# Two groups of matmul operands of an encoder kernel get new places in SBUF: the gated outputs 64 bytes lower and the memory's tiles 32 bytes higher, modulo 256

## Chip, cores and metric

The kernel runs on one core of a Trainium2 chip, in one launch. The metric is the device time of the whole program in microseconds. A version is timed in several runs on the same chip, and the median counts.

## What is computed

The reference is an encoder trunk of two layers over 256 positions of width 2048. In each layer a pre-normalized input `h` is projected by one large matrix into mixer columns, cross-attention queries and a gate. The mixer is a multi-scale mean with a grouped matrix in layer 0, and a gated DeltaNet in both directions over chunks of 64 in layer 1. Beside it stands a cross-attention of 4 heads into 256 memory tokens.

```python
for i in range(DEPTH):
    h = rmsnorm(x, norm_w[i])
    kv = rmsnorm(mem, mem_norm_w[i]) @ w_kv_mem[i]
    ...
    if i % 2 == 0:
        y = pooling_branch(h, pool_w_in[j], pool_w_group[j], pool_scale[j], mem_k, mem_v)
    else:
        y = deltanet_branch(h, dn_w_in[j], dn_conv_w[j], dn_a_log[j], dn_dt_bias[j], dn_norm_w[j],
                            mem_k, mem_v)
    x = x + y @ w_out[i]
return rmsnorm(x, final_norm_w)
```

Both branches return the concatenation of the mixer's and the attention's output times `silu(gate)`. This product is what the title calls the gated outputs.

## The kernel before

All activations lie transposed, with features on the 128 partitions and the 256 positions along the free axis. Each dense product runs in float32r, with every operand split into a high part and a remainder. For one 128x128 block of weights TensorE therefore runs three matmuls of 256 columns: high weights by high input, high weights by the input's remainder, remainder of the weights by high input. Each is a weight load (LDWEIGHTS, engine PEld in the profile) and a matmul (PE). The weights come in from HBM as 512 KB pieces (`wr`), ScalarE rounds them to `wh` (L226) and VectorE forms the remainder `wl` (L228). `wh` and `wl` have three buffers each, `wr` four.

The streamed operands of the dense products are three kinds of tiles of 128 x 2 x 256 float32, which is 2048 bytes in a partition, the first half the high part and the second half the remainder:

- `xs`, 16 tiles: the normalized input of a layer (`h`).
- `y`, 12 tiles: the gated outputs, streamed by `out_piece` against `w_out`.
- `ms`, 16 tiles: the memory's normalized tokens, and in layer 0 the pooled mixer input. The same pool tag also gives room for small tiles of the attention and of the decay chain (`xq`, `xp`, `xpt`, `cnt`, `pacc` and others).

For the memory's values (`wv`) the roles are exchanged: there `wh` and `wl` are streamed with 512 columns, and `ms` is the loaded operand.

The order of the work on TensorE and on the DMA queue of SyncE is written out by the program itself. A list of jobs and waiting tasks (`Flow`) is played against an estimated clock, and each job yields every second block, so that the small matmuls of the attention and of the DeltaNet chains (`pa`, `kk`) stand between the dense ones.

Where a tile lies is decided by pools. Pools on the right side are laid out from the upper end of SBUF downwards in the order in which they are opened; before, that is `apad` (96 floats, so 384 bytes), `act` (with `xs` and `y`) and `mr` (with `ms`). Pools on the left side (`keep`, `work`, `mp`, later `gp`) are laid out upwards. In the built program `wh` and `wl` begin at byte 56480 and 68768 of a partition and have a length of 4096, so that every 128x128 block of them begins 160 bytes past a multiple of 256. `xs` (from 171616), `y` (from 204384) and `ms` (from 138848) all begin 96 past a multiple of 256, which is 64 below the weights.

Of the kernel before, what the change touches and what calls it, by code (L numbers as in the profile page):

```python
# [9 lines left out]
F32 = mybir.dt.float32  # L10
F32R = mybir.dt.float32r
# [6 lines left out]
P = 128  # L18
S = 256
# [14 lines left out]
SQ_BUFS = 3  # L34
SLICE = 2

A_PAD = 96

P_STAGE = 600
P_UA = 600  # L40
# [99 lines left out]
def trunk_kernel(  # L140
# [18 lines left out]
    nc = tc.nc  # L159
# [2 lines left out]

    keep = ctx.enter_context(tc.tile_pool(name="keep", bufs=1))
    work = ctx.enter_context(tc.tile_pool(name="work", bufs=2))
    apad = ctx.enter_context(tc.tile_pool(name="apad", bufs=1, side="right"))
    nc.gpsimd.memset(apad.tile([P, A_PAD], F32, name="apad"), 0.0)
    act = ctx.enter_context(tc.tile_pool(name="act", bufs=1, side="right"))
    psd = ctx.enter_context(tc.tile_pool(name="psd", bufs=PS_DENSE, space=PSUM))
    psa = ctx.enter_context(tc.tile_pool(name="psa", bufs=PS_CHAIN, space=PSUM))
# [5 lines left out]
    def xt(dt):  # L175
        return act.tile([P, 2, S], dt, tag="xs", name="xs", bufs=KT)
# [243 lines left out]
        return g  # L420

    def new_y(last=False):
        return xt(F32R) if last else act.tile([P, 2, S], F32R, tag="y", name="y", bufs=12)

    def out_piece(src, ys, nk, *flags, acc=None, done=None):
        per = HC // nk
# [74 lines left out]
    def attention(layer, wsrc, ct_q, ct_g, xready, kvready):  # L501
# [22 lines left out]
        def g_jobs(h):  # L524
            for kk in range(4):
                def post(ps, kk=kk):
                    ct = 4 * h + kk
                    g = gate_of(ps)
                    po = pa(S)
                    for mt in range(2):  # L530
                        mm(po, kv["v", layer][:, mt, ct * P : (ct + 1) * P], pT[h][:, mt, :], mt == 0, mt == 1)
                    yf = wt([P, S], F32, "yf", 2)
                    V.tensor_tensor(out=yf, in0=g, in1=po, op=ALU.mult)  # L533
                    ys[h][kk] = new_y()
                    split_to(ys[h][kk], yf)
                    if kk == 3:
                        yflag[h].set(flow.now + 2500)

                dense([wsrc[ct_g + 4 * h + kk, i] for i in range(2)], get_xs, post, soft[h])
# [2 lines left out]

    mp_cm = tc.tile_pool(name="mp", bufs=1)
    mp = mp_cm.__enter__()
    mr_cm = tc.tile_pool(name="mr", bufs=1, side="right")
    mr = mr_cm.__enter__()
    mem_ready, mem_done, x_ready, kv_ready = Flag(), Flag(), Flag(), Flag()

    def start_up():
# [67 lines left out]
    def mix_jobs(g):  # L617
        gates = [None] * 8

        def gate_job(c):  # L620
            def post(ps):
                gates[c] = gate_of(ps)

            dense([pw_d[48 + 8 * g + c, i] for i in range(2)], get_xs, post)

        def mix_job(c):
            def post(ps):
                ct = 8 * g + c
                yf = wt([P, S], F32, "yf", 2)
                V.scalar_tensor_tensor(  # L630
                    out=yf, in0=ps, scalar=scale_h[:, ct : ct + 1], in1=gates[c], op0=ALU.mult, op1=ALU.mult
                )
                py[g][c] = new_y()
                split_to(py[g][c], yf)
                if c == 7:
                    pyflag[g].set(flow.now + 2500)

            dense([pg_d[g, c]], lambda: pooled[g], post, pflag[g])

        gate_job(0)  # L640
        for c in range(8):
            if c < 7:
                gate_job(c + 1)
            mix_job(c)
# [459 lines left out]
    def norm_chain(g, os, so, crq):  # L1104
# [37 lines left out]
        for n in range(4):  # L1142
            yf = wt([P, S], F32, "yf", 2)
            V.tensor_tensor(out=yf, in0=os[n // 2][:, n % 2, :], in1=g_tiles[g][n], op=ALU.mult)
            y_tiles[g][n] = new_y(g == 7)
            split_to(y_tiles[g][n], yf)
# [86 lines left out]
    engines = ENGINES  # L1233
    with tc.manual_schedule(engines=engines):
        flow.run(len(flow.jobs) - n_first)
    mr_cm.__exit__(None, None, None)
    mp_cm.__exit__(None, None, None)
    gp = ctx.enter_context(tc.tile_pool(name="gp", bufs=1))
    gpool.append(gp)
# [159 lines left out]
```

## Time and profile before

| | |
|---|---|
| median of three runs | 2534.39 us |
| the three runs | 2524.43, 2534.39, 2536.51 us |
| the profiled execution, its own time | 2533.24 us |
| its span, first to last instruction | 2531.5 us |
| mean granted TensorE clock | 0.996 |
| PE busy, share of the span | 2501.1 us, 99% |
| PEld busy | 2446.8 us, 97% |
| DVE busy | 1785.2 us, 71% |
| ACT busy | 1237.5 us, 49% |
| mean share of the DMA engines on the weights' queue | 51.7% |

The span is the time from the first to the last instruction of the profiled execution, 1.7 us less than its own time. PE's busy time is a union of overlapping matmuls: one matmul takes some 280 ns from start to end, but the next one starts some 115 ns after it. How fast TensorE works is therefore read from the number of matmuls in a stretch of time, not from its busy share.

### The profile page before, as it was taken

The page shows a single profiled execution, that of the slowest core. Times are in us where ns is not written, and L with a number is a line of the kernel's source. Part 1 is how long each engine was busy: PE and PEld are TensorE (multiplying, and loading weights), DVE is VectorE, ACT ScalarE, POOL GpSimd, SP SyncE. Part 2 cuts the span into 40 slices and gives each one's busy share as a digit, 9 for nine tenths or more (in the row PEclk, how much of TensorE's full clock was granted, in tenths as well). Part 3 has the DMA queues.
Part 4 walks back from the last instruction along what each step waited for, and adds up shares of the span by engine and source line. Part 5 has one row for each costly group of instructions (what it writes and reads, how often), then busy time and mean ns, then how long its engine had stood idle before and what let it go on. Part 6 is the DMA issues. An engine that isn't in the chain of part 4 may idle for free.

```text
span 2531.5 us, 53006 instructions
## 1 busy us (share of the span) xinstructions
PE 2501.1 (99%) x21996; PEld 2446.8 (97%) x21996; DVE 1785.2 (71%) x3317; ACT 1237.5 (49%) x1946; POOL 15.6 (1%) x45
## 2 busy tenths in 40 slices
PE   8999999999999999999999999999999999999998
PEld 7999999999999999988999999999999999999998
DVE  6574555657567585674546558979889797979886
ACT  6544444444444444554344446455555555564645
POOL 0000000000000000000000000000000000000000
PEclk9999999999999999999999999999999999999999
DMA  7655455666565555655564545435344443535352
GB/s 245 222 190 168 162 177 169 195 193 199 193 192 194 187 188 185 216 191 191 193 197 159 171 165 169 161 111 171 126 153 146 143 162 129 175 130 167 124 182 101
DMA packets 120817, 436.17 MB, mean 172 GB/s; under 512 B 13728, under 2 KB 13984, under 8 KB 120576
## 3 DMA queue, kind: packets, MB, share of 16 engines
q1 hardware_dynamic: 118080, 426.06, 51.7%
q0 software_dynamic: 1776, 5.64, 0.7%
q8 instruction: 172, 2.82, 0.4%
q10 hardware_dynamic: 720, 1.08, 0.1%
q14 instruction: 69, 0.57, 0.1%
HBM read 430.63 MB, written 2.10 MB: 171 GB/s over the span
## 4 chain that ended last, share of the span: by engine, by line
PE 94%; DVE 4%; ACT 1%; issue 1%; DMA 0%; DVEq 0%
PE pd L192 84%; PE pa L192 9%; DVE wl L228 2%; PE kk L192 1%; ACT wh L226 1%; PE pa L196 0%; DVE itmp L1003 0%; DVE Ti L1009 0%; DVE cacc L805 0%; DVE ms L356 0%; DVE Dg L993 0%; DVE L L995 0%; DVE o L1275 0%; DMA wr<-in_wv_dram 0%; DVE N L1013 0%
## 5 line engine op out<-in xcount | busy, mean ns | idle before, releaser
L228 DVE TENSOR_TENSOR wl<-wr,wh 128x1024 fp32r<-128x1024 f32 x802 | 981.7, 1224 | 568.2 <-ACT wh L226 565.9
L226 ACT CAST wh<-wr 128x1024 fp32r<-128x1024 f32 x802 | 842.7, 1051 | 960.7 <-PE pd L192 782.0
L192 PE MATMUL pd<-xs,wh 128*128 128x256 f32 x7328 | 1306.5, 282 | 3.6 <-DVE gt L419 2.8
L192 PEld LDWEIGHTS pd<-xs,wh 128*128 128x128 f32 x7328 | 1116.9, 189 | 8.5 <-DVE gt L419 3.0
L192 PE MATMUL pd<-xs,wl 128*128 128x256 f32 x3664 | 1021.2, 279 | 0.0
L192 PEld LDWEIGHTS pd<-xs,wl 128*128 128x128 f32 x3664 | 694.2, 189 | 0.4 <-DVE wl L228 0.2
L192 PE MATMUL pd<-y,wh 128*128 128x256 f32 x2944 | 510.9, 278 | 1.2 <-DVE y L266 1.2
L192 PEld LDWEIGHTS pd<-y,wh 128*128 128x128 f32 x2944 | 445.6, 188 | 1.7 <-DVE y L266 1.4
L192 PE MATMUL pd<-y,wl 128*128 128x256 f32 x1472 | 409.0, 278 | 0.0
L192 PEld LDWEIGHTS pd<-y,wl 128*128 128x128 f32 x1472 | 277.8, 189 | 0.5 <-DVE wl L228 0.4
L192 PE MATMUL pd<-ms,wh 128*128 128x256 f32 x1536 | 264.8, 277 | 0.0
L192 PEld LDWEIGHTS pd<-ms,wh 128*128 128x128 f32 x1536 | 232.0, 188 | 0.2
L192 PE MATMUL pd<-ms,wl 128*128 128x256 f32 x768 | 212.7, 277 | 0.0
L192 PE MATMUL pd<-wh,ms 128*128 128x512 f32 x512 | 161.3, 395 | 6.2 <-ACT ms L355 6.2
L192 PEld LDWEIGHTS pd<-ms,wl 128*128 128x128 f32 x768 | 144.7, 188 | 0.0
L805 DVE SCALAR_TENSOR_TENSOR cacc<-cu,small,cacc 128x256 f32<-128x256 f32 x256 | 122.5, 482 | 5.7 <-ACT cacc L803 1.3
L192 PEld LDWEIGHTS pd<-wh,ms 128*128 128x128 f32 x512 | 96.8, 189 | 26.5 <-ACT ms L355 6.2
L455 DVE TENSOR_TENSOR xT<-xT,pd 128x512 f32<-128x512 f32 x140 | 96.1, 686 | 35.7 <-PE pd L192 35.5
L192 PE MATMUL pd<-wl,ms 128*128 128x512 f32 x256 | 101.1, 395 | 0.3 <-DVE wl L228 0.2
L1003 DVE TENSOR_TENSOR itmp<-L,Ti 128x126 f32<-128x126 f32 (+22 forms) x248 | 63.3, 255 | 2.3
L1009 DVE TENSOR_TENSOR Ti<-Ti,itmp 128x126 f32<-128x126 f32 (+22 forms) x248 | 63.3, 255 | 2.2
L265 ACT CAST y<-yf 128x256 fp32r<-128x256 f32 x92 | 35.9, 405 | 55.9 <-DVE yf L533 54.1
(218 smaller groups left out, 1780.9 us busy)
## 6 DMA issues: line engine op xcount, KB each, us to landing
wr<-in_dw_dram SPq DMA_DIRECT2D x258, 512.0 KB, 3.5
wr<-in_pw_dram SPq DMA_DIRECT2D x192, 512.0 KB, 3.5
wr<-in_wo_dram SPq DMA_DIRECT2D x192, 512.0 KB, 3.5
wr<-in_wv_dram SPq DMA_DIRECT2D x64, 512.0 KB, 4.1
wr<-in_wk_dram SPq DMA_DIRECT2D x64, 512.0 KB, 4.2
wr<-in_pg_dram SPq DMA_DIRECT2D x32, 512.0 KB, 3.8
xs<-in_mem_dram SPq DMA_DIRECT2D x8, 256.0 KB, 6.9
xT<-in_x_dram SPq DMA_DIRECT2D x4, 512.0 KB, 5.8
```

Source lines behind the costliest of these rows:

```text
L192: T.matmul(out, lhsT=lhsT, rhs=rhs, start=start, stop=stop)
L226: A.copy(out=hi, in_=raw)
L228: V.tensor_tensor(out=lo, in0=raw, in1=hi.bitcast(F32), op=ALU.subtract)
L265: A.copy(out=dst[:, 0, :], in_=src)
L455: V.tensor_tensor(out=xv, in0=xv, in1=pss[0], op=ALU.add)
L805: V.scalar_tensor_tensor(out=a, in0=u[:, k : k + S], scalar=cwh[:, ct, k : k + 1], in1=a, op0=ALU.mult, op1=ALU.add)
L1003: V.tensor_tensor(out=tv, in0=L[:, j + 1 : 32, j : j + 1].to_broadcast([P, n, c]), in1=Ti[:, j : j + 1, 0:c].to_broadcast([P, n, c]), op=A ...
L1009: V.tensor_tensor(out=Ti[:, j + 1 : 32, 0:c], in0=Ti[:, j + 1 : 32, 0:c], in1=tv, op=ALU.subtract)
```

## The change

Three pads take the place of one. `pad0` (48 floats) stands above a pool of its own for `y`, `acty`; `pad1` (48 floats) stands between it and `act`, which now holds `xs` alone; `pad2` (56 floats) stands between `act` and `mr`.

```diff
-A_PAD = 96
+
+PADS = (48, 48, 56)
...
-    apad = ctx.enter_context(tc.tile_pool(name="apad", bufs=1, side="right"))
-    nc.gpsimd.memset(apad.tile([P, A_PAD], F32, name="apad"), 0.0)
+    def pad(stack, i):
+        pool = stack.enter_context(tc.tile_pool(name=f"pad{i}", bufs=1, side="right"))
+        nc.gpsimd.memset(pool.tile([P, PADS[i]], F32, name=f"pad{i}"), 0.0)
+
+    pad(ctx, 0)
+    acty = ctx.enter_context(tc.tile_pool(name="acty", bufs=1, side="right"))
+    pad(ctx, 1)
     act = ctx.enter_context(tc.tile_pool(name="act", bufs=1, side="right"))
...
-        return xt(F32R) if last else act.tile([P, 2, S], F32R, tag="y", name="y", bufs=12)
+        return xt(F32R) if last else acty.tile([P, 2, S], F32R, tag="y", name="y", bufs=12)
...
-    mr_cm = tc.tile_pool(name="mr", bufs=1, side="right")
-    mr = mr_cm.__enter__()
+    mr_cm = ExitStack()
+    pad(mr_cm, 2)
+    mr = mr_cm.enter_context(tc.tile_pool(name="mr", bufs=1, side="right"))
...
-    mr_cm.__exit__(None, None, None)
+    mr_cm.close()
```

What the pools make of it, in bytes within a partition:

| tile | begins at, before | modulo 256 | begins at, after | modulo 256 | after, against the weights |
|---|---|---|---|---|---|
| `wh`, `wl` (each block) | 56480, 68768 | 160 | the same | 160 | |
| `xs` | 171616 | 96 | the same | 96 | 64 below |
| `y` | 204384 | 96 | 204576 | 32 | 128 away |
| `ms` and what shares its tag | 138848 | 96 | 138624 | 128 | 32 below |

The tiles on the left side stay where they were. On PE, VectorE, ScalarE and the DMA queue of SyncE the instructions, their order and what each waits for are the same before and after. On GpSimd the `apad` memset gives way to three memsets. The first fence has GpSimd's rows of the program before around its start, the second those of the program after.

```order
L1394 UNCONDITIONAL_BRANCH
L166 MEMSET apad 128x96
L208 MEMSET epsc 128x1
L575 MEMSET ub_93 128x8
L576 MEMSET ub_93 128x8
```

```order
L1401 UNCONDITIONAL_BRANCH
L168 MEMSET pad_64 128x48
L168 MEMSET pad_72 128x48
L214 MEMSET epsc 128x1
L168 MEMSET pad_101 128x56
L582 MEMSET ub_106 128x8
L583 MEMSET ub_106 128x8
```

Behind these rows GpSimd's list goes on as before. Nothing that computes has moved in time order; only addresses differ.

## Rows read from the trace of the kernel before

**Rows 1.** The page: busy time of engines, and the chain that ended last.

```profile
PE 2501.1 (99%) x21996; PEld 2446.8 (97%) x21996; DVE 1785.2 (71%) x3317; ACT 1237.5 (49%) x1946; POOL 15.6 (1%) x45
...
PE 94%; DVE 4%; ACT 1%; issue 1%; DMA 0%; DVEq 0%
PE pd L192 84%; PE pa L192 9%; DVE wl L228 2%; PE kk L192 1%; ACT wh L226 1%; PE pa L196 0%; DVE itmp L1003 0%; DVE Ti L1009 0%; DVE cacc L805 0%; DVE ms L356 0%; DVE Dg L993 0%; DVE L L995 0%; DVE o L1275 0%; DMA wr<-in_wv_dram 0%; DVE N L1013 0%
```

**Rows 2.** The chain in order of time, 430 to 1110 us: start, length, work.

```profile
436.39 0.86 PE pa L192 x4
437.26 617.83 PE pd L192 x5361
```

**Rows 3.** Weight loads in two stretches: length, busy time (count), clock, DMA share, GB/s.

```profile
440.00:790.00 350.00, 350.00 (x3090) 1.00 0.60 193
800.00:1055.00 255.00, 255.00 (x2166) 1.00 0.60 193
```

**Rows 4.** Groups by form within 440 to 790 us: PE, then PEld.

```profile
L192 PE MATMUL pd<-xs,wl 128*128 128x256 f32 x633 | 174.7, 276 | 0.0
L192 PE MATMUL pd<-y,wl 128*128 128x256 f32 x270 | 74.5, 276 | 0.0
L192 PE MATMUL pd<-ms,wl 128*128 128x256 f32 x128 | 35.3, 276 | 0.0
...
L192 PEld LDWEIGHTS pd<-xs,wl 128*128 128x128 f32 x632 | 118.6, 188 | 0.0
```

**Rows 5.** The same groups within 800 to 1055 us.

```profile
L192 PE MATMUL pd<-xs,wh 128*128 128x256 f32 x768 | 136.3, 281 | 0.0
L192 PE MATMUL pd<-xs,wl 128*128 128x256 f32 x384 | 107.9, 281 | 0.0
...
L192 PE MATMUL pd<-y,wl 128*128 128x256 f32 x215 | 60.4, 281 | 0.0
...
L192 PE MATMUL pd<-ms,wl 128*128 128x256 f32 x123 | 34.6, 281 | 0.0
...
L192 PEld LDWEIGHTS pd<-xs,wl 128*128 128x128 f32 x384 | 73.7, 192 | 0.0
```

**Rows 6.** The page's costliest groups, whole run: busy, mean ns, idle before.

```profile
L226 ACT CAST wh<-wr 128x1024 fp32r<-128x1024 f32 x802 | 842.7, 1051 | 960.7 <-PE pd L192 782.0
...
L192 PE MATMUL pd<-xs,wl 128*128 128x256 f32 x3664 | 1021.2, 279 | 0.0
...
L192 PE MATMUL pd<-y,wh 128*128 128x256 f32 x2944 | 510.9, 278 | 1.2 <-DVE y L266 1.2
...
L192 PE MATMUL pd<-y,wl 128*128 128x256 f32 x1472 | 409.0, 278 | 0.0
...
L192 PE MATMUL pd<-ms,wh 128*128 128x256 f32 x1536 | 264.8, 277 | 0.0
...
L192 PE MATMUL pd<-ms,wl 128*128 128x256 f32 x768 | 212.7, 277 | 0.0
L192 PE MATMUL pd<-wh,ms 128*128 128x512 f32 x512 | 161.3, 395 | 6.2 <-ACT ms L355 6.2
...
L265 ACT CAST y<-yf 128x256 fp32r<-128x256 f32 x92 | 35.9, 405 | 55.9 <-DVE yf L533 54.1
```

**Rows 7.** Timeline of PEld around 1672 us: start, length, load, count.

```profile
1671.90 1.87 PEld L192 LDWEIGHTS pa<-cst,osq 128*128 128x128 f32 x16
1673.69 0.19 PEld L192 LDWEIGHTS kk<-kq 128*128 128x128 f32 x1
```

**Rows 8.** Timeline of PE, 66 to 71 us; between the rows the same three repeat.

```profile
66.22 0.62 PE L192 MATMUL pd<-wh,ms 128*128 128x512 f32 x2
66.68 0.39 PE L192 MATMUL pd<-wl,ms 128*128 128x512 f32 x1
...
70.34 0.62 PE L192 MATMUL pd<-wh,ms 128*128 128x512 f32 x2
```

**Rows 9.** Groups of GpSimd over the whole run.

```profile
L1252 POOL MEMSET tt<- 128x512 f32 x2 | 1.0, 546 | 0.0
...
L166 POOL MEMSET apad<- 128x96 f32 x1 | 0.2, 178 | 0.3 <-POOLq L1384 0.3
```

## Prediction

> **What bounds the kernel now.** The page comes first, for the engine that never rests: PE is busy for 99% of the span and holds 94% of the chain that ended last, 84% with the dense products alone [rows 1]. The chain in order of time then says whether TensorE waits for its operands. It has one unbroken piece of 617.83 us with 5361 dense matmuls [rows 2]. ScalarE, the first step of the weights' staging, waits 782.0 us for TensorE to free buffers [rows 6]. So weights are early, and a dense stretch is as long as its matmuls times their pitch, the time from one start to the next.
>
> The pitch is read from counts in stretches without other work. From 440 to 790 us 3090 weight loads go by in 350 us, 113.3 ns each; from 800 to 1055 us 2166 in 255 us, 117.7 ns each [rows 3]. The granted clock is 1.00 in both, which is the level of 2.4 GHz. Staging, waits and operands are of the same kind in both. What differs stands in the groups by form: in the first stretch a matmul takes 276 ns from start to end, whether it streams `xs`, `y` or `ms`, and in the second 281 ns for all three; the load of `wl` takes 188 ns in the first and 192 in the second [rows 4, 5]. So there are two rhythms, quick and slow, 4.4 ns apart. A rhythm holds for hundreds of microseconds and goes on unbroken from one kind of streamed tile to another. All three kinds lie at the same place against the weights.
>
> How much of the run is slow follows from the mean lengths. For `y` it is 278 ns, which is two fifths of the way from 276 to 281; for `ms` 277, one fifth; for `xs` with `wl` 279, three fifths [rows 6]. As these are whole nanoseconds, each share may be off by a tenth, and matmuls that follow a break lengthen the means too.
>
> **What a pitch is made of.** 256 columns at 2.4 GHz are 106.7 ns, so the quick rhythm loses 6.6 ns and the slow one 11.0. Two rows give floors. Sixteen weight loads whose matmuls stream one column each start at 1671.90 us and the next load at 1673.69, 112 ns a load [rows 7]: the load itself keeps a pitch from going below 112, and the quick rhythm stands 1.3 ns above that. And the attention's plain float32 matmuls, each a pass of 256 columns, go by at 0.86 us for four, 215 ns each [rows 2]; that is two clocks a column (512 clocks are 213 ns) and next to nothing lost. So the loss belongs to float32r streams, which fetch a column at every clock while the next weights are fetched from the same memory, and a dependence on where the two lie is possible. The memory's values, where `wh` and `wl` are streamed against loaded `ms`, lie 64 above instead of 64 below: six groups of three from 66.22 to 70.34 us are 228.9 ns each for 512 columns, 114.4 per 256 [rows 8], between the two rhythms.
>
> **The change part by part.**
>
> *Memsets.* One memset of 178 ns goes and three smaller come [rows 9]. GpSimd is busy for 15.6 us in all [rows 1], and nothing waits for the pads. That costs nothing; without cover it would be three times 178 ns, half a microsecond.
>
> *Elementwise work on the moved tiles.* VectorE and ScalarE write `y` and `ms` at other addresses, with the same shapes. I cost this at nothing, since `wh` waits for TensorE far longer than it works late; were each of the 92 splits of `y` 50 ns longer on either engine, 5 us of work would stand against ScalarE's 960.7 us of idle time before `wh` [rows 6].
>
> *The streamed tiles.* 4416 matmuls stream `y` (2944 and 1472), 2304 stream `ms` (1536 and 768) and 768 load it in exchanged roles (512 in the row and half as many with `wl`) [rows 6]. No row shows a float32r product of this form at the two new places, so the pitch there is bounded from both sides. Below: the weight load's 112. From the present mix to quick throughout saves 0.4 x 4416 x 4.4 = 7.8 us on `y` and 0.2 x 2304 x 4.4 = 2.0 us on `ms`; from quick to 112 a further 6720 x 1.3 = 8.7 us; and if the 768 wide ones fell from 228.9 to the 215 of the float32 passes, 768 x 13.9 = 10.7 us. Together 29 us. Above: slow throughout costs 0.6 x 4416 x 4.4 + 0.8 x 2304 x 4.4 = 11.7 + 8.1 = 19.8 us, and one more step of 4.4 ns on all 6720 would add 29.6.
>
> *The tiles that stay.* `xs` has 10992 of the matmuls (three times the 3664 with `wl`) and keeps its place, but not its neighbours. Today a rhythm passes through a change of kind, since nothing about the addresses changes there. Afterwards each change of kind also changes the place. A slow stretch can then end where a `y` or `ms` stretch begins, and so can a quick one. In the stretch of [rows 5], 768 + 384 = 1152 matmuls of `xs` are slow between such changes, 1152 x 4.4 = 5.1 us.
>
> At one point the Trainium skill speaks against all this. TensorE: Matmul & The Clock Gate, in "Step-by-step: what each phase is for", says that TensorE has two independent SBUF read ports, one for the streamed operand and one for the weight load, so that loading the next weights takes no read bandwidth from the running matmul. By that rule the two rhythms have nothing to do with addresses, and the sum is zero. The trace neither confirms nor refutes it: the slow stretch has both the longer matmul and the longer load of `wl` [rows 5].
>
> Which value I take: quick throughout for `y` and `ms`, not the floor, because 276 ns is the best that any long stretch shows [rows 4]; the wide ones unchanged, being at 114.4 per 256 columns already at a place unlike the others [rows 8]; and one slow stretch of `xs` cut. **The sum:** 7.8 + 2.0 + 5.1 = 14.9 us less than the profiled execution's own 2533.24, which is 2518. That execution lies 1.2 us below the median of 2534.39.
>
> **The rivals.**
>
> *The place does not matter.* The rhythm would be an accident of timing after each break, which changes with any small shift. For it: the wide matmuls at another place cost the same per column [rows 8], and the three runs differ by 12 us, as 2750 matmuls changing rhythm would make (12 us / 4.4 ns). Against it: float32 passes lose nothing [rows 2]. Time: 2533, with 8 us of play on either side. This is also the case in which the change does not do what it is made for, and the one that the skill's rule gives.
>
> *Slow at the new places.* `y` at 128 and `ms` at 32 would fall into the slow rhythm each time and leave it only where `xs` begins. It decides from about 2900 further slow matmuls on (12.7 us / 4.4 ns). For it: nothing ties the quick rhythm to these places, and one stretch of 255 us shows that slow can hold through every kind [rows 3, 5]. Against it: `y` and `ms` are quick more often than slow [rows 6]. Time: 2533 + 20 = 2553; with `xs` drawn along, its two fifths of quick matmuls at 4.4 ns are 19 us more, 2572.
>
> *Below the quick rhythm.* At the new places the loss falls away as in the float32 passes, and the weight load's 112 bounds. All of the 29 us gives 2504, with the `xs` stretch 2499, and more if further slow stretches of `xs` are cut. Against it: no long float32r stretch stands below 113.3.
>
> **How the numbers follow.** Quick throughout at 2518: 0.35. No effect: 0.29. Slow: 0.21. Below quick: 0.13. Something else: 0.02. The predicted time is 2518. The likeliest case alone runs from 2508 (all `xs` stretches of that kind cut) to 2524 (`ms` and `xs` unchanged). For eight in ten the range reaches to 2494 below, past the floor's 2499, and to 2554 above, over the slow case without `xs`; what is left out is most of the slow case with `xs` and a larger fall.
>
> About 0.5%, 12.7 us, is what a measurement of this kernel can tell from no change, by the spread of its three runs. Faster by more than that (under 2521.7) takes 0.27 of the first case, 0.12 of the floor and 0.02 of the play: 0.41. Within it are the rest of the first, most of the second and a partly slow `y`: 0.38. Slower is the bulk of the slow case and a mishap: 0.21.
>
> **What would show it.** Right: matmuls with `y` and `ms` at 276 or 277 ns in the groups of the whole run, `wl` loads of 188 ns beside them, the mean of `xs` with `wl` at 278 or less, and the counts in stretches of `y` alone at 8.8 per microsecond. The wide matmuls still at 229 would confirm the third choice. Wrong: a whole-run mean of 281 or more for `y` or `ms` (the slow rival), below 275 (the floor), or unchanged means with the end within 8 us of before (no effect). I would be wrong by a size, too, if `xs` changed its share of slow matmuls as a whole, for each tenth of it is 4.8 us.

## The result and the profile after

The changed kernel takes 2553.37 us (median of four runs, 2550.68 to 2555.91) against 2533.0 for the kernel before (median of four, 2524.43 to 2536.51): a ratio of 1.0085, 95% interval 1.0058 to 1.0113. It is slower. The profiled execution took 2553.65 us, its span is 2551.9; that is 20.4 us over the profiled execution of before.

The page of the changed kernel shows TensorE as full as before and its chain fuller; lines of the code are shifted by six or seven.

```profile
PE 2524.9 (99%) x21996; PEld 2469.0 (97%) x21996; DVE 1786.2 (70%) x3317; ACT 1236.8 (48%) x1946; POOL 15.7 (1%) x47
...
PE 96%; DVE 2%; ACT 1%; issue 0%; DMA 0%; DVEq 0%; POOL 0%
...
L232 ACT CAST wh<-wr 128x1024 fp32r<-128x1024 f32 x802 | 842.1, 1050 | 989.9 <-PE pd L198 819.4
L198 PE MATMUL pd<-xs,wh 128*128 128x256 f32 x7328 | 1302.4, 281 | 3.5 <-DVE gt L425 2.8
...
L198 PE MATMUL pd<-xs,wl 128*128 128x256 f32 x3664 | 1019.6, 278 | 0.0
...
L198 PE MATMUL pd<-y,wh 128*128 128x256 f32 x2944 | 528.1, 282 | 0.6 <-DVE y L272 0.6
...
L198 PE MATMUL pd<-y,wl 128*128 128x256 f32 x1472 | 414.5, 282 | 0.0
...
L198 PE MATMUL pd<-ms,wh 128*128 128x256 f32 x1536 | 274.0, 281 | 0.0
...
L198 PE MATMUL pd<-ms,wl 128*128 128x256 f32 x768 | 215.7, 281 | 0.0
L198 PE MATMUL pd<-wh,ms 128*128 128x512 f32 x512 | 164.0, 399 | 6.1 <-ACT ms L361 6.1
```

The loads of `wl` beside `y`, which take 192 ns in the slow rhythm of before [rows 5], are short here:

```profile
L198 PEld LDWEIGHTS pd<-y,wl 128*128 128x128 f32 x1472 | 277.2, 188 | 0.0
```

Against [rows 6] the matmuls that stream `y` went from 278 to 282 ns, those that stream `ms` from 277 to 281, the wide ones that load `ms` from 395 to 399. The staging of weights is unchanged (1050 ns for `wh` against 1051) and ScalarE waits longer for TensorE, 819.4 us against 782.0. So no other engine is the cause. For an engine that is never idle a longer matmul is a longer pitch: 4 ns x 4416 = 17.7 us for `y`, 4 x 2304 = 9.2 for `ms`, 4 x 768 = 3.1 for the wide ones, 30.0 in all. `xs` gave back some of it: its 10992 matmuls keep TensorE busy for 1335.8 us, against 1340.1 before, 4.3 less. TensorE's idle time, the span less its busy time, fell from 30.4 to 27.0 us. 30.0 less 4.3 less 3.4 is 22.3, near the 20.4 measured; the lengths are rounded to whole nanoseconds.

Counts of weight loads in stretches of one kind alone show the two places side by side. The columns are those of [rows 3]; the first, third and fourth stretch stream `xs`, the second `y`. A count includes loads that stand across an edge, one or two in 340, so a pitch read from 40 us comes out 0.4 to 0.8 ns short.

```profile
446.00:486.00 40.00, 40.00 (x354) 1.00 0.60 191
490.00:530.00 40.00, 40.00 (x338) 1.00 0.58 185
603.00:643.00 40.00, 40.00 (x354) 1.00 0.61 200
916.00:955.00 39.00, 39.00 (x345) 1.00 0.62 198
```

`xs` goes by in 40 / 354 = 113.0 ns, `y` right behind it in 118.3, at the same granted clock of 1.00 (2.4 GHz); from start to start in the trace it is 113.4 and 118.7. The rhythm no longer passes through a change of kind. It is `ms` that ends a slow stretch: behind each of the 29 stretches of `ms` in this trace (20 matmuls or more) `xs` goes by at 113.4 to 114.0 ns, whereas behind `y`, at 533, 689, 845 and 1001 us, it is slow (117.8) until the next `ms`. So `xs` is mostly quick in the stretch behind 800 us, too, in which before all kinds were slow [rows 3, 5]. The changed kernel's groups within 800 to 1055 us:

```profile
L198 PE MATMUL pd<-xs,wl 128*128 128x256 f32 x368 | 102.0, 277 | 0.0
...
L198 PE MATMUL pd<-y,wl 128*128 128x256 f32 x255 | 71.8, 281 | 0.0
...
L198 PE MATMUL pd<-ms,wl 128*128 128x256 f32 x108 | 30.3, 281 | 0.0
```

### The profile page after: what moved, and what is told of

Read it like the earlier page. It is cut to its first block, busy times and chain, and to the rows that moved or that the text cites. A ratio compares the mean times of both kernels' runs of the same rounds, so it can differ in the third digit from the quotient of the medians.

```text
span 2551.9 us, 53008 instructions
## 1 busy us (share of the span) xinstructions
PE 2524.9 (99%) x21996; PEld 2469.0 (97%) x21996; DVE 1786.2 (70%) x3317; ACT 1236.8 (48%) x1946; POOL 15.7 (1%) x47
## 4 chain that ended last, share of the span: by engine, by line
PE 96%; DVE 2%; ACT 1%; issue 0%; DMA 0%; DVEq 0%; POOL 0%
PE pd L198 86%; PE pa L198 9%; PE kk L198 1%; DVE wl L234 1%; PE pa L202 0%; ACT wh L232 0%; DMA xs<-in_mem_dram 0%; DVE cacc L812 0%; DVE o L1282 0%; DMA wr<-in_wv_dram 0%; DVE Dg L1000 0%; DVE itmp L1010 0%; DVE ms L362 0%; DVE Ti L1016 0%; DVE L L1002 0%
## 5 line engine op out<-in xcount | busy, mean ns | idle before, releaser
L232 ACT CAST wh<-wr 128x1024 fp32r<-128x1024 f32 x802 | 842.1, 1050 | 989.9 <-PE pd L198 819.4
L198 PE MATMUL pd<-y,wh 128*128 128x256 f32 x2944 | 528.1, 282 | 0.6 <-DVE y L272 0.6
L198 PEld LDWEIGHTS pd<-y,wh 128*128 128x128 f32 x2944 | 452.1, 188 | 1.1 <-DVE y L272 0.8
L198 PE MATMUL pd<-y,wl 128*128 128x256 f32 x1472 | 414.5, 282 | 0.0
L198 PE MATMUL pd<-ms,wh 128*128 128x256 f32 x1536 | 274.0, 281 | 0.0
```

Source lines behind the costliest of these rows:

```text
L198: T.matmul(out, lhsT=lhsT, rhs=rhs, start=start, stop=stop)
L232: A.copy(out=hi, in_=raw)
```

## Experiments

The theory after the result: the pitch of a float32r matmul depends on where its streamed tile lies against the weights, modulo 256 bytes, and 64 below is simply a better place than 128 away or 32 below. The rival: any shift throws the dice of the two rhythms anew, and this throw was a bad one. A second rival: it is the tile's own address that counts, not the distance to the weights.

All variants below set the three pads (for `y`, `xs`, `ms` in this order, in floats) and leave a pad out where it is 0; only the pads' sizes differ from the changed kernel unless more is shown. Where the pads alone move `xs`, it is by a whole 256 bytes. "Length" is the mean length of one matmul in the groups by form.

### Each kind alone

```diff
-PADS = (48, 48, 56)
+PADS = (48, 48, 0)
```

> Only the gated outputs y move to 128 bytes from the weights; ms stays 64 below. Place theory (the pitch of a float32r matmul depends on where its streamed tile lies against the weights): y means of 282 ns for one matmul as in the changed kernel, ms back at 277, and the time rises by y's share alone, about 16 us over before, 2549. Accident theory (any shift throws the dice of the quick and slow rhythms anew): y's mean is as likely as not near 278, ms anywhere between 276 and 281, time 2525 to 2541.

Measured: 2548.71 us against 2524.2, ratio 1.0079 (1.0048 to 1.0111). The groups of the whole run:

```profile
L200 PE MATMUL pd<-xs,wl 128*128 128x256 f32 x3664 | 1022.1, 279 | 0.0
...
L200 PE MATMUL pd<-y,wl 128*128 128x256 f32 x1472 | 414.7, 282 | 0.0
...
L200 PE MATMUL pd<-ms,wl 128*128 128x256 f32 x768 | 212.8, 277 | 0.0
```

```diff
-PADS = (48, 48, 56)
+PADS = (32, 0, 56)
```

> Only the memory's tiles move, to 32 below the weights; y and xs stay 64 below (both lie a whole 256 bytes elsewhere, which the place theory counts as the same place). Place theory: ms at 281 ns, the wide matmuls that load ms at 399, y and xs as before at 278 and 279, time up by 9 us for the streamed and 3.5 us for the wide ones, about 2545. Accident theory: time 2525 to 2541 and no tie of the slow rhythm to ms.

Measured: 2544.69 us, ratio 1.0070 (1.0048 to 1.0092).

```profile
L200 PE MATMUL pd<-y,wl 128*128 128x256 f32 x1472 | 408.7, 278 | 0.8 <-DVE wl L236 0.8
...
L200 PE MATMUL pd<-ms,wl 128*128 128x256 f32 x768 | 215.9, 281 | 0.0
L200 PE MATMUL pd<-wh,ms 128*128 128x512 f32 x512 | 163.3, 398 | 6.2 <-ACT ms L363 6.2
```

Each kind is slow where it was moved and as before where it was not. That is the place theory's pattern, and the ranges of the accident theory (up to 2541) are missed by both medians. The lengths carry this reading, not the times. The expected times were reckoned from a before of 2533, but the 22 runs beside these lie at 2522 to 2529 eighteen times and at 2533.7 to 2537.1 four times. Against their median the two rises are 24.5 and 20.5 us, 8 more each than the 16 and 12.5 that were priced, and that the medians fall on 2549 and 2545 is partly luck.

The two runs also show which move brings `xs` back to the quick rhythm. With `ms` alone moved, `xs` is quick behind each of its 29 stretches. With `y` alone moved, between 528 and 1060 us, a rhythm passes unbroken from the end of one `y` through `xs` and `ms` to the next `y`, and can be either. Three stretches of `xs` alone from that run:

```profile
600.00:640.00 40.00, 40.00 (x342) 1.00 0.60 191
755.00:795.00 40.00, 40.00 (x355) 1.00 0.61 187
912.00:952.00 40.00, 40.00 (x341) 1.00 0.59 186
```

The first and the last are slow, where the changed kernel has 354 loads in 40 us.

### Weights and streamed tiles shifted together

```diff
-PADS = (48, 48, 56)
+PADS = (48, 0, 0)
...
+    nc.gpsimd.memset(keep.tile([P, 48], F32, name="lpad"), 0.0)
     work = ctx.enter_context(tc.tile_pool(name="work", bufs=2))
```

`y`, `xs` and `ms` all lie at 32 modulo 256, `wh` and `wl` at 96.

> Weights and all three kinds of streamed tiles shift together by 64 bytes downwards modulo 256, by a pad of 192 bytes on the left side and a larger one on the right, so that every kind is 64 below the weights as before, while y lies at 32 modulo 256 as in the changed kernel. If the place against the weights counts: as before, y near 278 ns, 2533 within 8 us. If the absolute place of the streamed tile counts: y at 282, xs and ms slow as well, 2550 and more.

Measured: 2524.06 us, ratio 0.9997 (0.9979 to 1.0014).

```profile
L201 PE MATMUL pd<-xs,wl 128*128 128x256 f32 x3664 | 1018.9, 278 | 0.0
...
L201 PE MATMUL pd<-y,wl 128*128 128x256 f32 x1472 | 408.4, 277 | 0.8 <-DVE wl L237 0.8
...
L201 PE MATMUL pd<-ms,wl 128*128 128x256 f32 x768 | 212.2, 276 | 0.0
```

`y` lies at the very address modulo 256 that it has in the changed kernel, and is quick. So the absolute place is out, and the distance to the weights decides.

One rival is left by this: `wr`, `wh` and `wl`, which the DMA engines, ScalarE and VectorE write meanwhile, lie at the loaded weights' place too, so it could be their writes that disturb the stream. The changed kernel's trace speaks against it. Within stretches of `y` the pitch from start to start is 118.7 ns for 1935 matmuls beside which ScalarE does nothing and 118.8 for 1850 beside which it works throughout. It is 118.7 both with VectorE idle (502) and at work (3080), and both with no DMA packet under way (736) and with sixteen or more (1135).

### Around the circle

```diff
-PADS = (48, 48, 56)
+PADS = (0, 32, 0)
```

> y lies 64 above the weights, xs and ms 64 below. This is 128 away from y's place before, so a pattern that repeats every 128 bytes makes y as before: 278 ns, 2533. With a pattern of 256 bytes y has a pitch of its own. By the wide matmuls of before, which stream weights lying 64 above the loaded tile at 114.4 ns per 256 columns, it would be between the rhythms, near 278 ns again; if the rest of the circle is slow, 281 or 282 and about 2547. Accident theory: 2525 to 2541.

Measured: 2540.32 us, ratio 1.0057 (1.0042 to 1.0071), so a pattern that repeats every 128 bytes is out. The median lies within the accident theory's range as well, but the stretches of `y` do not: twelve of the thirteen longest go by at 117.8 or 118.1 ns from start to start, one at 114.6.

```profile
L200 PE MATMUL pd<-y,wh 128*128 128x256 f32 x2944 | 522.6, 280 | 1.4 <-DVE y L274 1.1 <-DVE gt L427 0.3
L200 PE MATMUL pd<-y,wl 128*128 128x256 f32 x1472 | 410.8, 279 | 0.0
```

Four further runs: two put `y` and `ms` at other places (pads 16, 16, 8; then 56, 40, 40), a third exchanged the places of the change (24, 8, 16), and a fourth took two more places (8, 24, 48).

> One step of a map around the circle of 256 bytes: y at the weights' own place (0), ms 96 below, xs 64 below as always. Place theory with 64 below as the best place: a matmul of y takes 280 ns or more, of ms 278 or more, and the time is above before's 2524 by 4400 and 2300 times the added pitch, some 15 to 25 us. If 64 below is only one of several good places, one of the two stays at 276 to 278. A conflict that is worst where streamed tile and weights begin in the same place would make y here the slowest of all, 283 or more.

> Map: y 96 above the weights, ms 32 above, xs 64 below. By the y run at 64 above (279 to 280 ns for one matmul, 117.5 of pitch) and the changed kernel's at 128 (282, 118.8), y here lies between them, 280 to 282. ms 32 above is open: 276 if good places repeat, 281 if not. Time 2535 to 2550.

> The change with its two kinds exchanged: y 32 below the weights, ms 128 away. If the place alone sets the pitch, whichever kind of tile lies there, y takes what ms took in the changed kernel (281 ns, pitch 118.2) and ms what y took (282, 118.8), and the time is again near 2550. If the kind matters, one of them goes back to 277 or 278.

> Map: y 32 above the weights, ms at the weights' own place, xs 64 below. Place theory: y takes what ms takes at 32 above in the run before, within 1 ns, and ms what y takes at 0. Time 2530 to 2555, by these pitches.

Measured, beside 2524.85 of before: 2559.04 us (ratio 1.0130, 1.0097 to 1.0163), 2552.85 (1.0102, 1.0066 to 1.0137), 2557.9 (1.0125, 1.0091 to 1.0159) and 2546.94 (1.0084, 1.0058 to 1.0111). The first three are 10, 3 and 8 us above what was expected, and `y` in the second has 283 ns where 280 to 282 was expected. From the first and the fourth, `y` at the weights' own place and then `ms` there:

```profile
L200 PE MATMUL pd<-y,wl 128*128 128x256 f32 x1472 | 417.2, 283 | 0.0
```

```profile
L200 PE MATMUL pd<-y,wl 128*128 128x256 f32 x1472 | 411.7, 280 | 0.1
L200 PE MATMUL pd<-ms,wh 128*128 128x256 f32 x1536 | 277.5, 283 | 0.0
L200 PE MATMUL pd<-ms,wl 128*128 128x256 f32 x768 | 217.6, 283 | 0.0
```

All lengths of matmuls with `wl` loaded, by place (bytes above the weights, modulo 256; where several runs have a place, the values in the order of their kernels). The last column is the pitch from start to start in the long stretches of one moved kind alone:

| place | `y`, ns | `ms`, ns | pitch, ns |
|---|---|---|---|
| 128 away | 282 (changed), 282 | 283 | 118.7, in some 120.0 |
| 96 below | | 281 | 118.7 |
| 64 below | 278 (before), 278, 277 | 277 (before), 277, 276, 277 | 113.3 or 117.8 |
| 32 below | 281 | 281 (changed), 281 | 118.3 |
| 0 | 283 | 283 | 120.0 |
| 32 above | 280 | 280 | 116.7 |
| 64 above | 279 | | 117.8, in one 114.6 |
| 96 above | 283 | | 120.0 |

Weight loads in 40 us of `y` alone show the same order. The rows are from five runs: 64 above, 32 above, 32 below, 0 and 96 above.

```profile
640.00:680.00 40.00, 40.00 (x342) 1.00 0.57 187
643.00:683.00 40.00, 40.00 (x345) 1.00 0.60 193
647.00:687.00 40.00, 40.00 (x340) 1.00 0.59 187
648.00:688.00 40.00, 40.00 (x335) 1.00 0.59 188
645.00:685.00 40.00, 40.00 (x335) 1.00 0.57 185
```

Three things follow. Where both kinds were tried at one place their lengths agree within 1 ns, so it is the place and not the kind of tile. A length is not a pitch: 64 above has the shorter matmuls (279 ns against 280) but the longer pitch (117.8 against 116.7) beside 32 above, so places are to be ranked by the pitch. And 64 below is the best of the eight places by its quick rhythm, 113.3 ns against 116.7 to 120.0; its slow rhythm, 117.8, is no better than 64 above. The guess that the weights' own place (0) is the very worst holds only together with 96 above. None of the eight places promises a kernel quicker than the one before. `xs` was not moved alone.

### The changed kernel once more

> The changed kernel once more, beside runs of the kernel before on the same chip, which lay at 2524 in the last sets with a fifth of them near 2536. If the changed kernel's 2553 is a property of its places, it is 2549 to 2556 again and 1.1% over before's 2524; if it was an unlucky draw of rhythms, some of its runs come under 2540.

Measured: 2553.75 us (2553.04 to 2555.38) against 2523.61 (2522.6 to 2533.56), ratio 1.0108 (1.0083 to 1.0132). It is no unlucky draw. The draws are with the kernel before: most of its runs are near 2523, some near 2535.

### One half of the weights moved

In the kernel before, a small pad between the buffers of `wh` and `wl` moves `wl` up by 64 bytes and in a second variant (48 floats) by 192, which is down by 64 modulo 256. What lies behind `wl` on the left side, among it tiles of the attention and of the chains, moves with it, but no other operand of the dense products. All streamed tiles stay 64 below `wh`.

```diff
                 hi = wt(shape, F32R, "wh", W_SPLIT_BUFS)
+                if i == 0:
+                    nc.gpsimd.memset(wt([P, 16], F32, "wpad", 1), 0.0)
```

> All streamed tiles and wh stay as in the kernel before; wl alone moves up by 64 bytes, so that every streamed tile lies 128 away from wl and 64 below wh. Of three matmuls one has wl loaded, and another one streams while wl is being fetched for the next. If the place against the weights being fetched counts, the matmuls that lengthen are half of those with wh (the remainder's stream), so their mean rises by about 2 to 3 ns, and the group with wl stays near 278. If the place against the weights already loaded counts, the wl group goes to 282 or more and the wh group stays. In both cases about 5900 matmuls lose 5 ns, 2545 to 2555. If neither counts, only the place against wh, 2524.

> wl alone moves down by 64 bytes, to where the streamed tiles begin modulo 256 (place 0 against wl, 64 below wh). Place 0 was the slowest with 119.8 of pitch in the map. If the fetched weights count, the mean of the wh group rises and the wl group stays; if the loaded ones count, the wl group alone rises to 283. Time 2545 to 2560 in both, 2524 if wl does not matter.

Measured: 2579.19 us (ratio 1.0207, 1.0183 to 1.0232) and 2580.21 (1.0213, 1.0183 to 1.0242). Groups of the first, then of the second:

```profile
L192 PE MATMUL pd<-xs,wh 128*128 128x256 f32 x7328 | 1335.3, 285 | 2.9 <-DVE gt L421 2.2 <-ACT xs L267 0.7
L192 PE MATMUL pd<-y,wh 128*128 128x256 f32 x2944 | 525.8, 283 | 0.9 <-DVE y L268 0.9
L192 PE MATMUL pd<-y,wl 128*128 128x256 f32 x1472 | 411.7, 280 | 0.0
```

```profile
L192 PE MATMUL pd<-y,wh 128*128 128x256 f32 x2944 | 523.9, 282 | 0.8 <-DVE y L268 0.8
L192 PE MATMUL pd<-y,wl 128*128 128x256 f32 x1472 | 414.0, 281 | 0.0
```

The place against `wl` counts as well as the place against `wh`, and moving `wl` costs more than either reckoning said (56 us, not 20 to 35), since `xs` lengthens too (282 to 285 with `wh`). Both groups lengthen, the one with `wh` more (278 to 283 and 282, against 278 to 280 and 281), where each theory wanted one to stay. The starts in the traces tell the three matmuls of a block apart. In the first variant, within `y`, the pitch of the `wh` matmul beside which `wl` begins to be fetched is 119.5 ns, that of the other `wh` matmul 119.0, and that of the `wl` matmul 116.2, against 114.7 to 114.8 for all three before; in the second they are 118.0, 117.8 and 117.5. So the loss is not confined to the matmul that streams while the moved weights are fetched, nor to the one that has them loaded. Whether it is handed on from one matmul to the next stays open.

## Why the prediction was wrong

**What bounds the kernel** was right: the whole change is one of the pitch, TensorE is as full as before, and no other engine's row moved.

**The price of the memsets and the elementwise work** was right at nothing: the pads' memsets are not in the chain, the splits of `y` take 406 ns against 405, and `wh` takes 1050 against 1051.

**The step that failed** is "Which value I take: quick throughout for `y` and `ms`". I took the best pitch of the old place for the new ones, on the ground that no long stretch showed a better or a worse one than 276 and 281. The stretches of [rows 4, 5] had all been seen at one place and could not speak for another. The runs show that the new places have pitches of their own: by the starts `y` has 118.7 ns and `ms` 118.3, where the old place had 113.3 or 117.8. The term 7.8 + 2.0 us of gain became 17.7 + 9.2 of loss.

**"The wide ones unchanged"** failed too, with a small size: 395 to 399 ns, 3.1 us. I had read their 114.4 ns per 256 columns as the price of another place, 64 above [rows 8]. But a stream of 512 columns with exchanged roles does not speak for one of 256: tiles streamed from 64 above have a pitch of 117.8 ns, and of 114.6 in one stretch.

**The term for `xs`** was right in sign and near in size, 5.1 us against 4.3 of busy time, and its mechanism was right for `ms` and not for `y`. A slow stretch ends at the next `ms` at its new place, and with `y` alone moved it went on behind 800 us. Behind `y` a slow stretch of `xs` begins in four places. That the stretch was slow in the profile of before was itself a draw (see below).

**The rival that came true** is "slow at the new places", with 2553. Its size was partly luck: it priced `y` and `ms` at 19.8 us where 26.9 were lost, left out 3.1 for the wide ones, and let `xs` gain nothing. Its mechanism was right in that `y` and `ms` are slow each time and `xs` begins anew, though only behind `ms`. It is not the slow rhythm of before into which they fall: their pitch is longer than its 117.8 ns, and the loads of `wl` beside `y` take 188 ns, not 192. The rival "the place does not matter" fell: a shift of all operands together costs nothing (ratio 0.9997), a shift of one kind against the weights costs 0.6 to 0.8%. The Trainium skill's page TensorE: Matmul & The Clock Gate says in "Step-by-step: what each phase is for" that loading the next weights takes no read bandwidth from the running matmul. This case's traces differ: the pitch depends on where the streamed tile lies against the weights, from 113.3 to 120.0 ns, and the measurement decides.

Two ends of the likeliest case do not follow from its terms: with `ms` and `xs` unchanged it comes to 2525, not 2524, and no row gives the 2508. Neither bears on the forecast.

**The accident I had seen** is real, but it is a property of one place, not a substitute for it. With everything 64 below, a long stretch can be quick or slow. The variant with all operands shifted has the stretch behind 800 us quick, in an execution of 2524.02 us:

```profile
440.00:790.00 350.00, 350.00 (x3090) 1.00 0.61 193
800.00:1040.00 240.00, 240.00 (x2120) 1.00 0.63 197
```

That is 113.2 ns where the profile of before had 117.7 [rows 3]; 2166 matmuls at 4.4 ns are 9.5 us, about the distance between the profiled 2533.24 and the usual 2524. No profile of a usual run of the kernel before was kept, so that its time hangs on this stretch is argued, not shown. The profile that I priced against was in any case one of the slower draws, and against the usual one the change costs 30 us, 1.1%.

## What to carry to other kernels

Where TensorE bounds a kernel with float32r products of 256 columns, the place of the streamed tiles against the weights modulo 256 bytes can be worth a per cent, as it was here, and a pad finds it; 64 below the weights was best for both kinds that were moved. A place is a pair, so moving either side can cost: check both, and the remainder's buffers too, whenever a pool in front of them changes its size. Count matmuls in a stretch, for their mean length can rank two places the wrong way round. And a price read from stretches that all share one setting bounds nothing for another setting: if every row has the same place, the unknown place is open on both sides, and the best row says nothing about it.

## What the runs showed of the hardware that was not expected

The dependence itself: for 256 columns in float32r the mean length of a matmul runs from 276 to 283 ns and the pitch from 113.3 to 120.0 around a circle of 256 bytes, with the best place at 64 below the weights, and it follows the distance and not the address (ratio 0.9997 for a common shift). The other engines and the DMA have no part in it that the trace shows (118.7 ns with and without them). At the weights' own place the load of the weights lengthens as well. In the run with `y` there, the weight loads beside `y` and beside `xs` are:

```profile
L200 PEld LDWEIGHTS pd<-xs,wl 128*128 128x128 f32 x3664 | 693.0, 189 | 0.0
...
L200 PEld LDWEIGHTS pd<-y,wl 128*128 128x128 f32 x1472 | 282.8, 192 | 0.0
```

At the best place two rhythms are possible, 113.3 and 117.8 ns, within one execution at the same granted clock of 1.00. The times of one program fall into two groups as well (2522 to 2529 us in eighteen of 22 runs, 2533.7 to 2537.1 in four), which fits a rhythm that differs from run to run. What starts the slow one there is open in the kernel before; in the changed kernel it starts behind `y` in four places.
